# Expert routing beside a streamed projection: fewer and partly bfloat16 operations, maxima from the finished map, more steps a load

## The chip, the core and the metric

The kernel runs on one core of a Trainium2 chip. The metric is the time of one execution in microseconds of the device, taken as the median of several runs. The core has five engines with a queue each: TensorE (PE in the profile, its weight loads PEld), VectorE (DVE), ScalarE (ACT), GpSimd (POOL) and SyncE (SP, which here only issues DMAs). An engine executes its queue in order and waits at semaphores for the others.

## What is computed

One layer of a diffusion backbone for 256 latent tokens (and 256 context tokens) of width 2048: modulated RMSNorm, one input projection into an mLSTM and a differential attention, a gated merge, an output projection with residual, and then PEER, a retrieval among 128 x 128 = 16384 single-neuron experts. All work around the change lies in PEER:

```
q = (h @ w_pq).reshape(B, T, 8 heads, 2, 128)
s = einsum('bthpd,hpnd->bthpn', q, sub_keys)            # 128 scores per head and half
s1, i1 = top_k(s[..., 0, :], 16);  s2, i2 = top_k(s[..., 1, :], 16)
cand_s = s1[..., :, None] + s2[..., None, :]             # 256 candidates per head
top_s, pos = top_k(cand_s, 16)                           # 16 experts per head
idx = (i1 * 128 + i2)[pos];  g = softmax(top_s)
act = gelu(einsum('td,ted->te', h, expert_u[idx]))       # 128 experts per token
out = einsum('te,ted->td', g * act, expert_v[idx])
```

The result goes through a gated residual and a last RMSNorm.

## The kernel before

The kernel does not gather `expert_u`. It multiplies all 16384 rows of it with all 256 tokens ("the U stage"), and builds in the meantime a map of the gates, 16384 x 256, which is zero wherever a token did not choose an expert. The product of both weighs the rows of `expert_v` ("the V stage"). Of `expert_v` only those rows are read that some token of a group uses; which ones is worked out by `lists`.

The U stage is the loop `for i1 in range(0, P, 2)` over 64 pairs of key rows (from L1616). `u_pair` takes four pieces of 128 x 1024 float32 for a pair with `take()`: a piece is loaded by a DMA on SP's queue (L117), rounded to `hi` on ACT (L133), and its rest `lo` is subtracted on DVE, every fourth time on POOL (L136). `raw`, `hi` and `lo` have three buffers each. Then come 16 matmuls for the piece, eight with `hi` and 512 columns and eight with `lo` and 256 (L93, tile `s`), held in program order by `mp_`. After a pair DVE adds the halves (L1625), ACT takes the GELU (L1626), and ACT's queue writes the 128 x 512 result to `ag_dram` in DRAM (L1630).

Everything else in this stage is a chain of Python generators in the list `back`, begun by what `best` has left to do and then `plan`. After each piece `pump(pace[0])` runs `pace[0]` steps on average, where a step goes to the next `yield`. So `pace` and the `yield`s fix where the matmuls of the routing lie between those of U, since both are kept in program order; so are the DMAs of U's pieces, the gate map's and the gathers, each on its queue. The remaining instructions are placed by a planner with a time model of its own, which may move an instruction of DVE, ACT or POOL ahead of others that are not ready. The steps of `plan`:

- `best`: scores of the halves on PE, and their 16 best with `top16` (MAX8, FIND_INDEX8, MATCH_REPLACE8, twice).
- `retrieve(t)` for each of two tiles of 128 tokens: sums of candidates on POOL (L1170), `top16` over 256, softmax, and the two indices of each choice, found by a comparison with 0..15 (L1194, DVE), a product (L1196, POOL) and a sum (L1200, DVE); three transposes bring them to `i1T`, `i2T`, `gT` (L1207, L1208).
- `gate_map(t)`: for each token a matmul of two one-hots (`one_hots`, L1234), four tokens to a step. ACT makes the first one-hot with Abs and Relu (L1237, L1238), DVE and POOL in turn the second, which carries the gate (L1241). ACT copies the result from PSUM to the tile `gates` (L1279); DVE takes its maximum over the four tokens (L1283) and merges it into `most` for the group of 32 tokens (L1285). `gate_map(0)` is woven with `retrieve(1)`.
- `map_out`: each half of a map (64 tokens) leaves in eight DMAs of 512 KB on SP's queue (L1253), in pieces of 256 bytes, beside the next half; the last is run out by `plan`.
- `lists`: from `most`, which blocks of expert rows are needed and where they go: ten `fill`s (matmuls with triangular and full ones, scans on DVE, products on POOL), then one-hots for 126 columns, four to a step (L1408, L1409 on DVE, L1411 on ACT, L1412 on POOL), and 126 matmuls that add them up to index lists.
- `soon`: fetches eight blocks of `expert_v` by indirect DMAs on POOL's queue (L1501), waits until `made[0]` has reached `EARLY` = 104 slices of U, and then does the first five items of the V stage.

At the 63rd pair `drain()` runs all that is left of `plan`. The paces are 1.05 (L1448), 1.6 for the fills (L1461), 1.15 for the one-hots of `lists` (L1415) and 1.3 for `soon` (L1464).

## Time and profile before

| | us |
|---|---|
| timed runs, median of 3 (lowest to highest) | 2327.84 (2323.7 to 2328.26) |
| profiled execution, its own time | 2340.29 |
| its span, first to last instruction | 2338.4 |
| PE busy in the span | 2198.0 |
| DVE busy | 1570.3 |
| ACT busy | 1057.4 |
| POOL busy | 935.0 |
| U's first and last matmul start at | 1168.1 and 2048.6 |

The profile is of one execution. Busy is the time in which an engine's instructions run, one after another or overlapped. Of an instruction that waited, the trace names the one that released it ("<-"). Matmuls are pipelined, so two that follow each other overlap in the rows. An instruction is named by its line in the kernel; U's matmuls and those of the routing share L93, since both go through `mp_`, and are told apart by their tiles (`s` for U, `g` for the routing, `v` for the V stage).

### The profile page before, as it was taken

To read this page: it belongs to the slowest core of one execution; us is meant where nothing else is said; L and a number is where in the kernel's file an instruction comes from. 1 tells how busy PE (TensorE), PEld (TensorE's weight loads), DVE (VectorE), ACT (ScalarE), POOL (GpSimd) and SP (SyncE) were. 2 spreads that over 40 slices of the span, in tenths; PEclk is the share of its full clock that TensorE was granted. 3 is DMA by queue.
4 is the path that set the end of the run, shared out by engine and by line. 5 is a ranking of instruction groups with operands and counts; after the bars stand their busy time and mean duration, and the time that the engine had idled before them with its cause. 6 is when DMAs were issued, how large, how long until landed. Compare 5 with 4: busy or idle time off the path is not lost.

```text
span 2338.4 us, 37404 instructions
## 1 busy us (share of the span) xinstructions
PE 2198.0 (94%) x14184; PEld 1880.2 (80%) x14184; DVE 1570.3 (67%) x2760; ACT 1057.4 (45%) x1723; POOL 935.0 (40%) x957
## 2 busy tenths in 40 slices
PE   6999999999999999998999999999999989999994
PEld 3669988999899999887987888888787776756661
DVE  3357973767876858746799766876799944454553
ACT  3232232244566744444444777995335433333431
POOL 2132210236534200002235755772456454566553
PEclk9999999999999999998999999999999999999997
DMA  9968964866456588755556457878665588899895
GB/s 380 351 212 304 332 228 134 316 206 192 144 150 203 169 280 283 272 191 176 172 174 209 160 183 222 229 213 238 197 194 172 184 330 321 330 414 387 333 395 190
DMA packets 235910, 570.98 MB, mean 244 GB/s; under 512 B 85154, under 2 KB 118739, under 8 KB 221264
## 3 DMA queue, kind: packets, MB, share of 16 engines
q1 hardware_dynamic: 153888, 339.34, 44.1%
q0 software_dynamic: 46992, 211.67, 25.1%
q10 hardware_dynamic: 34848, 17.57, 2.6%
q8 instruction: 111, 1.82, 0.3%
q14 instruction: 71, 0.58, 0.1%
HBM read 524.33 MB, written 38.93 MB: 241 GB/s over the span
## 4 chain that ended last, share of the span: by engine, by line
PE 69%; DVE 12%; DMA 6%; issue 5%; ACT 3%; POOL 2%; ACTq 0%; another core or an unknown queue 0%; SPq 0%; DVEq 0%; POOLq 0%
PE acc L289 24%; PE s L93 18%; PE acc L278 11%; PE v L93 9%; DVE lo L136 4%; DMA raw<-expert_u 3%; PE g L93 2%; ACT hi L133 2%; PE m L433 1%; DMA vraw<-expert_v,idxV 1%; PE m L278 1%; DMA raw<-w_mod 1%; DVE at L1409 1%; DVE act L1625 1%; PE m L382 1%
## 5 line engine op out<-in xcount | busy, mean ns | idle before, releaser
L133 ACT CAST hi<-raw 128x1024 fp32r<-128x1024 f32 x528 | 551.6, 1048 | 803.9 <-PE acc L289 256.7
L136 DVE TENSOR_TENSOR lo<-raw,hi 128x1024 fp32r<-128x1024 f32 x457 | 599.7, 1316 | 283.6 <-ACT hi L133 279.2
L93 PE MATMUL s<-h,hi 128*128 128x512 f32 x2048 | 743.3, 404 | 3.2 <-ACT hi L133 2.6
L93 PE MATMUL s<-h,lo 128*128 128x256 f32 x2048 | 581.3, 284 | 33.2 <-DVE lo L136 20.8
L93 PEld LDWEIGHTS s<-h,hi 128*128 128x128 f32 x2048 | 388.6, 190 | 96.0 <-ACT hi L133 6.3
L93 PEld LDWEIGHTS s<-h,lo 128*128 128x128 f32 x2048 | 390.7, 191 | 45.5 <-DVE lo L136 28.6
L289 PE MATMUL acc<-hL,hi 128*128 128x256 f32 x2048 | 421.7, 286 | 0.0
L289 PEld LDWEIGHTS acc<-hL,hi 128*128 128x128 f32 x2048 | 342.5, 193 | 1.5
L289 PE MATMUL acc<-hL,lo 128*128 128x256 f32 x1024 | 292.3, 286 | 4.6 <-DVE lo L136 4.6
L136 POOL TENSOR_TENSOR lo<-raw,hi 128x1024 fp32r<-128x1024 f32 x71 | 176.9, 2492 | 254.3 <-ACT hi L133 248.6
L289 PEld LDWEIGHTS acc<-hL,lo 128*128 128x128 f32 x1024 | 197.5, 193 | 6.2 <-DVE lo L136 5.5
L117 POOL DMA_DIRECT2D raw<-w_mod x128 | 68.2, 533 | 300.2 <-DVE raw L522 278.7
L522 DVE SCALAR_TENSOR_TENSOR raw<-raw,cr 128x1024 f32<-128x1024 f32 x128 | 154.7, 1219 | 32.4 <-DMA raw<-w_mod 17.6
L1241 POOL TENSOR_SCALAR o<-iota,i1T,gT 128x128 f32<-128x128 f32 x128 | 138.9, 1092 | 93.1 <-PE g L93 49.3
L1517 DVE TENSOR_TENSOR lo<-vraw,hi 128x1024 fp32r<-128x1024 f32 x74 | 90.3, 1228 | 100.5 <-ACT hi L1515 76.1
L1501 POOL DMA_INDIRECT vraw<-expert_v,idxV x99 | 106.6, 1077 | 97.7 <-PE v L93 38.1
L289 PE MATMUL acc<-hC,hi 128*128 128x256 f32 x512 | 134.0, 283 | 0.0
L1515 ACT CAST hi<-vraw 128x1024 fp32r<-128x1024 f32 x74 | 77.1, 1049 | 115.0 <-PE v L93 56.1
L93 PE MATMUL v<-hi,l 128*128 128x512 f32 x448 | 123.5, 394 | 4.0 <-issue 3.1
L1625 DVE TENSOR_REDUCE act<-s 128x256 f32<-128x512 f32 x126 | 86.2, 684 | 53.6 <-PE s L93 48.2
L1501 POOL DMA_INDIRECT ag<-ag_dram,idxG x99 | 106.3, 1074 | 33.6 <-issue 27.3
L93 PE MATMUL v<-vraw,w 128*32 128x512 f32 x640 | 90.2, 642 | 28.5 <-DVE w L1536 12.9
(427 smaller groups left out, 3859.9 us busy)
## 6 DMA issues: line engine op xcount, KB each, us to landing
raw<-expert_u SPq DMA_DIRECT2D x256, 512.0 KB
raw<-w_in SPq DMA_DIRECT2D x176, 512.0 KB
raw<-w_mod POOLq DMA_DIRECT2D x128, 512.0 KB
raw<-w_mod SPq DMA_DIRECT2D x64, 512.0 KB
raw<-w_out SPq DMA_DIRECT2D x32, 512.0 KB
raw<-w_pq SPq DMA_DIRECT2D x32, 512.0 KB
ag_dram<-gates SPq DMA_DIRECT2D x32, 512.0 KB
ag_dram<-act ACTq DMA_DIRECT2D x126, 128.0 KB
```

The source lines that it names most:

```text
L93: tc.keep_in_program_order(mm(*args, **kw))
L117: d = queue.dma_start(r, src)
L133: nc.scalar.copy(h, r)
L136: (nc.vector if shared[0] else nc.gpsimd).tensor_tensor(l, r, h.bitcast(F32), op=OP.subtract)
L278: mm(acc[ti], lhsT=lhs(sa, ti, 2 * kp + k2), rhs=hl[sb][:, k2 * 512:(k2 + 1) * 512], start=first and k2 == 0 and i == 0, stop=last and k2 ...
L289: mm(acc[c][:, g * T:(g + 1) * T], lhsT=hl[sb][:, k2 * 512 + c * P:k2 * 512 + (c + 1) * P], rhs=rhs(sa, g, k), start=first and k2 == 0 and ...
L522: product = nc.vector.scalar_tensor_tensor(r, r, 1.0, cr, op0=OP.mult, op1=OP.mult, accum_out=part[:, h, i:i + 1])
L1241: (nc.gpsimd if i % 2 else nc.vector).tensor_scalar(o2[:, i, 0:width], iota[:, 0:width], cols[:, i:i + 1], factor[:, i:i + 1], op0=OP.is_e ...
L1501: tc.keep_in_program_order(nc.gpsimd.indirect_dma_start(out=out, out_offset=None, in_=src, in_offset=bass.IndirectOffsetOnAxis(ap=idx[:, b ...
L1515: nc.scalar.copy(h, raw)
L1517: nc.vector.tensor_tensor(l, raw, h.bitcast(F32), op=OP.subtract)
L1625: nc.vector.reduce_sum(act[:, e], ps.rearrange("p s t -> p t s"), axis=AX.X)
```

## The change

- `top16` yields after its first round. In `retrieve` a step therefore ends in the middle of a head; in `best` nothing changes.
- `retrieve` looks up the two indices without POOL: positions and indices are copied to bfloat16 with the heads innermost, and for each of the two indices DVE compares 16 x 16 x 8 elements, multiplies as many, and adds in a tree of 1024, 512, 256 and 128 elements. It has 17 steps in place of 23.
- `one_hots`: all four second one-hots of a group are made on DVE (two on DVE and two on POOL before). The first one-hot is made on ACT for every second group, for the others by one comparison of 512 elements on DVE.
- The maxima for `most` are no longer taken from PSUM for each group of four tokens. `map_out` takes them from the finished tile `gates`, 16 rows and two groups of 32 tokens at a time (1024 elements), right after the DMA of these rows. `map_out` has 8 steps and a last one in place of 16 and one, and is stepped at every second group, from the second on.
- `lists`: the sums over kinds in `fill` become additions in bfloat16; the one-hots are in bfloat16 with the four columns innermost, both operands too, and the product with `column` is on DVE instead of POOL. The matmuls read their four columns with a step of four elements. `hots` always makes four columns; the last group overlaps the one before.
- `pace` is 1.3 from the beginning (1.05 before) and 1.7 for the one-hots of `lists` (1.15 before).

```diff
@@ top16, best
             if r == 0:
                 nc.vector.match_replace(src, v, src, NEG)
+                yield
+
+    iota8 = tkr.tile([P, 16, HEADS], BF16, name="iota8")
+    nc.vector.tensor_copy(iota8, b3(iota[:, 0:16], HEADS))
...
@@ retrieve
-        tif = tk.tile([P, 16, 16], F32, name="tif", tag="tif", bufs=1)
-        nc.vector.tensor_copy(tif, ti[t])
+        tib = tk.tile([P, 2, 16, HEADS], BF16, name="tib", tag="tib", bufs=1)
+        nc.vector.tensor_copy(tib, ti[t].rearrange("p (h s) j -> p s j h", s=2))
...
-            top16(cs.rearrange("p a b -> p (a b)"), gv[:, h, :], gp[:, h, :])
-            yield
+            for _ in top16(cs.rearrange("p a b -> p (a b)"), gv[:, h, :], gp[:, h, :]):
+                yield
...
         nc.vector.tensor_tensor(e, e, b3(z, 16), op=OP.mult)
+        yield
...
-        posf = tk.tile([P, 2, HEADS, 16], F32, name="posf", tag="posf", bufs=1)
-        nc.vector.tensor_copy(posf, pos)
+        posb = tk.tile([P, 2, 16, HEADS], BF16, name="posb", tag="posb", bufs=1)
+        nc.vector.tensor_copy(posb, pos.rearrange("p s h k -> p s k h"))
         yield
         ii = []
+        every = [P, 16, 16, HEADS]
         for s in range(2):
+            oh = tk.tile(every, BF16, name="oh", tag="oh", bufs=1)
+            nc.vector.tensor_tensor(oh, posb[:, s].unsqueeze(1).to_broadcast(every),
+                                    iota8.unsqueeze(2).to_broadcast(every), op=OP.is_equal)
+            yield
+            nc.vector.tensor_tensor(oh, oh, tib[:, s].unsqueeze(2).to_broadcast(every), op=OP.mult)
+            yield
+            for w in (8, 4, 2):
+                nc.vector.tensor_tensor(oh[:, 0:w], oh[:, 0:w], oh[:, w:2 * w], op=OP.add)
             r = tk.tile([P, HEADS, 16], F32, name="ix", tag=f"ix{s}", bufs=1)
-            for h in range(HEADS):
-                if h % 4 == 0:
-                    four = tk.tile([P, 4, 16, 16], F32, name="oh", tag="oh", bufs=1)
-                oh = four[:, h % 4]
-                nc.vector.tensor_tensor(oh, b3(posf[:, s, h, :], 16),
-                                        iota[:, 0:16].unsqueeze(1).to_broadcast([P, 16, 16]), op=OP.is_equal)
-                nc.gpsimd.tensor_tensor(oh, oh, ti4[:, h, s, :].unsqueeze(1).to_broadcast([P, 16, 16]),
-                                        op=OP.mult)
-                if h % 4 == 3:
-                    yield
-                    nc.vector.reduce_sum(r[:, h - 3:h + 1], four, axis=AX.X)
-                if h % 2:
-                    yield
+            nc.vector.tensor_tensor(r.rearrange("p h k -> p k h"), oh[:, 0], oh[:, 1], op=OP.add)
             ii.append(r)
-        yield
+            yield
...
@@ one_hots
+        if on_act:
+            for i in range(4):
+                nc.scalar.activation(o1[:, i], iota, AF.Abs, bias=rows[:, i:i + 1], scale=-1.0)
+            nc.scalar.activation(o1, o1, AF.Relu, bias=ones[:, 0:1], scale=-1.0)
+        else:
+            nc.vector.tensor_tensor(o1, b3(rows, P), iota.unsqueeze(1).to_broadcast([P, 4, P]), op=OP.is_equal)
...
-        for i in range(n):
-            (nc.gpsimd if i % 2 else nc.vector).tensor_scalar(o2[:, i, 0:width], iota[:, 0:width], cols[:, i:i + 1], factor[:, i:i + 1],
+        for i in range(4):
+            nc.vector.tensor_scalar(o2[:, i], iota, cols[:, i:i + 1], factor[:, i:i + 1],
                                     op0=OP.is_equal, op1=OP.mult)
...
@@ map_out
-        for i in range(0, P, 8):
+        for i in range(0, P, 16):
             g, j = gates[i // 64], i % 64
-            if i % 16 == 0:
-                tc.keep_in_program_order(nc.sync.dma_start(rows[:, i:i + 16, w], g[:, j:j + 16, :]))
+            tc.keep_in_program_order(nc.sync.dma_start(rows[:, i:i + 16, w], g[:, j:j + 16, :]))
+            nc.vector.reduce_max(most[:, 4 * t + 2 * hf_:4 * t + 2 * hf_ + 2, i:i + 16].rearrange("p g i -> p i g"),
+                                 g[:, j:j + 16, :].rearrange("p i (g c) -> p i g c", g=2), axis=AX.X)
             yield
...
@@ gate_map
-            return one_hots(i2T[:, w], i1T[:, w], gT[:, w])
+            return one_hots(i2T[:, w], i1T[:, w], gT[:, w], q // 4 % 2)
...
-                top = most[:, 4 * t + at // 32 - (at % 32 == 0), :]
-                new = gm.tile([P, P], F32, name="new", tag="new", bufs=2) if (at - 4) % 32 else top
-                nc.vector.reduce_max(new, ps.rearrange("p t i -> p i t"), axis=AX.X)
-                if new is not top:
-                    nc.vector.tensor_tensor(top, top, new, op=OP.max)
-                step(leaving)
+                if q % 8:
+                    step(leaving)
                 yield
...
@@ lists, fill
-            nc.vector.reduce_sum(gone[:, 0:w], pw.rearrange("p c i -> p i c"), axis=AX.X)
+            if n == 4:
+                nc.vector.tensor_tensor(half_gone[:, :, 0:w], pw[:, 0:2], pw[:, 2:4], op=OP.add)
+                pw2 = half_gone[:, :, 0:w]
...
+                nc.vector.tensor_tensor(gone[:, 0:w], pw2[:, 0], pw2[:, 1], op=OP.add)
...
@@ lists, hots
+            i = min(i, N_LIST - 4)
+            w = slice(i, i + 4)
+            o1 = ls.tile([P, P, 4], BF16, name="h1", tag="h1", bufs=3)
+            o2 = ls.tile([P, 2, N_BLOCKS, 4], BF16, name="h2", tag="h2", bufs=3)
+            at = ls.tile([P, N_BLOCKS, 4], BF16, name="at", tag="at", bufs=2)
+            nc.vector.tensor_tensor(o1, hl[:, 1, w].unsqueeze(1).to_broadcast([P, P, 4]), iota4, op=OP.is_equal)
+            nc.vector.tensor_tensor(at, hl[:, 0, w].unsqueeze(1).to_broadcast([P, N_BLOCKS, 4]), iota4[:, 0:N_BLOCKS],
+                                    op=OP.is_equal)
+            nc.scalar.activation(o2[:, 0], at, AF.Copy, scale=row)
+            nc.vector.tensor_tensor(o2[:, 1], at, column[:, w].unsqueeze(1).to_broadcast([P, N_BLOCKS, 4]), op=OP.mult)
...
-        pace[0] = 1.15
+        pace[0] = 1.7
...
-                mp_(sums, lhsT=o1[:, j], rhs=o2[:, j], start=i + j == 0, stop=i + j == N_LIST - 1)
+            for j in range(max(0, i + 4 - N_LIST), 4):
+                mp_(sums, lhsT=o1[:, :, j], rhs=o2[:, :, :, j], start=i + j == 0, stop=i + 4 >= N_LIST and j == 3)
...
@@ plan
-    pace = [1.05]
+    pace = [1.3]
```

More of the change, by code (lines that the diff above doesn't have):

```diff
@@ L1140, in best @@
             for i in range(4):
-                top16(sc[:, i, :], tv[t][:, 4 * blk + i, :], ti[t][:, 4 * blk + i, :])
+                for _ in top16(sc[:, i, :], tv[t][:, 4 * blk + i, :], ti[t][:, 4 * blk + i, :]):
+                    pass
                 yield
@@ L1161, in retrieve @@
     def retrieve(t):
-        tif = tk.tile([P, 16, 16], F32, name="tif", tag="tif", bufs=1)
-        nc.vector.tensor_copy(tif, ti[t])
+        tib = tk.tile([P, 2, 16, HEADS], BF16, name="tib", tag="tib", bufs=1)
+        nc.vector.tensor_copy(tib, ti[t].rearrange("p (h s) j -> p s j h", s=2))
         tv4 = tv[t].rearrange("p (h s) i -> p h s i", s=2)
-        ti4 = tif.rearrange("p (h s) i -> p h s i", s=2)
         gv = tk.tile([P, HEADS, 16], F32, name="gv", tag="gv", bufs=1)
@@ L1231, in build, with one_hots @@
     i1T, i2T, gT = slots
-    def one_hots(rows, cols, factor, n=4, width=P):
+    def one_hots(rows, cols, factor, on_act):
         o1 = gm.tile([P, 4, P], F32, name="o1", tag="o1", bufs=3)
-        for i in range(n):
-            nc.scalar.activation(o1[:, i], iota, AF.Abs, bias=rows[:, i:i + 1], scale=-1.0)
-        nc.scalar.activation(o1[:, 0:n], o1[:, 0:n], AF.Relu, bias=ones[:, 0:1], scale=-1.0)
+        if on_act:
[4 more added lines that the diff above has]
+            nc.vector.tensor_tensor(o1, b3(rows, P), iota.unsqueeze(1).to_broadcast([P, 4, P]), op=OP.is_equal)
         o2 = gm.tile([P, 4, P], F32, name="o2", tag="o2", bufs=3)
-        for i in range(n):
-            (nc.gpsimd if i % 2 else nc.vector).tensor_scalar(o2[:, i, 0:width], iota[:, 0:width], cols[:, i:i + 1], factor[:, i:i + 1],
+        for i in range(4):
+            nc.vector.tensor_scalar(o2[:, i], iota, cols[:, i:i + 1], factor[:, i:i + 1],
                                     op0=OP.is_equal, op1=OP.mult)
@@ L1308, in lists @@
         nc.vector.tensor_scalar(row, row, 1.0, None, op0=OP.add)
+        iota4 = ls.tile([P, P, 4], BF16, name="iota4")
+        nc.vector.tensor_copy(iota4, b3(iota, 4))
         column = ls.tile([P, N_LIST], BF16, name="column")
@@ L1334, in lists @@
         nc.gpsimd.memset(places, 0.0)
-        gone = ls.tile([P, N_LIST], F32, name="gone")
+        gone = ls.tile([P, N_LIST], BF16, name="gone")
+        half_gone = ls.tile([P, 2, N_LIST], BF16, name="half_gone")
         blocks_at = ls.tile([P, 16, 4], F32, name="blocks_at")
@@ L1392, in lists @@
         placei = ls.tile([P, 3, N_LIST], I32, name="placei")
-        hl = ls.tile([P, 2, N_LIST], F32, name="hl")
-        nc.vector.reduce_sum(gone, places.rearrange("p c i -> p i c"), axis=AX.X)
-        nc.vector.tensor_scalar(placei[:, 2], gone, float(NOWHERE), None, op0=OP.add)
+        hl = ls.tile([P, 2, N_LIST], BF16, name="hl")
+        nc.vector.reduce_sum(zero, places.rearrange("p c i -> p i c"), axis=AX.X)
+        nc.vector.tensor_scalar(placei[:, 2], zero, float(NOWHERE), None, op0=OP.add)
         nc.vector.tensor_scalar(placei[:, 1], placei[:, 2], P - 1, None, op0=OP.bitwise_and)
@@ L1425, in lists @@
                 ready.append(hots(i + 8))
-            for j in range(min(4, N_LIST - i)):
-                mp_(sums, lhsT=o1[:, j], rhs=o2[:, j], start=i + j == 0, stop=i + j == N_LIST - 1)
+            for j in range(max(0, i + 4 - N_LIST), 4):
+                mp_(sums, lhsT=o1[:, :, j], rhs=o2[:, :, :, j], start=i + j == 0, stop=i + 4 >= N_LIST and j == 3)
             yield
```

15 lines of the change are left out of this document (5 added, 10 removed).

## The prediction

> **What bounds the kernel now.** I read the page first, then the windows of the U stage, beside which the routing runs: all engines (PE, PE's weight load, DVE, ACT and POOL busy, then granted clock, DMA share, GB/s), and PE's instructions on the tile `s`, which count U's matmuls.
>
> ```profile
> span 2338.4 us, 37404 instructions
> ...
> PE 69%; DVE 12%; DMA 6%; issue 5%; ACT 3%; POOL 2%; ACTq 0%; another core or an unknown queue 0%; SPq 0%; DVEq 0%; POOLq 0%
> ```
>
> ```profile
> 1168.00:1302.00 134.00, 122.64 (x686) 106.17 (x685) 122.35 (x306) 63.34 (x77) 72.67 (x58) 0.96 0.57 180
> 1302.00:1598.00 296.00, 291.67 (x1832) 260.20 (x1831) 213.56 (x358) 242.84 (x535) 186.24 (x182) 0.99 0.72 207
> 1598.00:1648.00 50.00, 45.83 (x251) 38.16 (x250) 26.83 (x36) 17.65 (x21) 7.19 (x3) 1.00 1.00 271
> 1648.00:1763.00 115.00, 108.37 (x601) 91.25 (x600) 103.39 (x133) 44.28 (x46) 61.24 (x41) 0.99 0.60 190
> 1763.00:1868.00 105.00, 99.06 (x610) 82.54 (x609) 100.71 (x106) 53.38 (x70) 56.65 (x40) 1.00 0.52 170
> 1868.00:2050.00 182.00, 168.31 (x988) 130.56 (x986) 78.43 (x106) 58.10 (x61) 90.19 (x69) 0.99 0.89 328
> ```
>
> ```profile
> 1168.00:1302.00 134.00, 119.90 (x655) 0.96 0.57 180
> 1302.00:1598.00 296.00, 249.00 (x1317) 0.99 0.72 207
> 1598.00:1648.00 50.00, 45.83 (x251) 1.00 1.00 271
> 1648.00:1763.00 115.00, 107.38 (x581) 0.99 0.60 190
> 1763.00:1868.00 105.00, 93.50 (x483) 1.00 0.52 170
> 1868.00:2050.00 182.00, 149.91 (x818) 0.99 0.89 328
> ```
>
> I call the rows A (scores, `retrieve(0)`), B (both gate maps, with `retrieve(1)`), C (the last map leaves), D (fills of `lists`), E (its one-hots), F (`soon`). PE sets the time, but DVE is nearly as full in A (91%), D (90%) and E (96%). What PE needs without waits comes from the chain of waits and from the groups:
>
> ```profile
> 1302.48 0.89 PE g L93 x8
> 1303.38 5.65 PE s L93 x32
> 1309.03 0.89 PE g L93 x8
> ```
>
> ```profile
> L93 PE MATMUL g<-skT,qT 128*128 128x128 f32 x24 | 3.2, 275 | 0.0
> L93 PE MATMUL v<-vraw,w 128*32 128x512 f32 x168 | 19.3, 596 | 0.0
> L93 PE MATMUL g<-h,h 128*128 128x198 bf16 x126 | 15.8, 251 | 1.9 <-DVE h L1408 1.9
> ```
>
> A *load* is one piece of U, 16 matmuls, 2.82 us; a group of four gate-map columns is 0.89. A: 655/16 loads are 115.5, with scores and transposes 119.5, so 14.5 of 134 are lost. B: 232 + 64 x 0.89 = 289, lost 7. C: 44.2, lost 5.8. D: 102.4 and about 4.6 for its small matmuls (an estimate), lost 8. E: 85.1 + 15.8, lost 4.1. F: 144 + 19, lost 19. The change adds and removes no matmul, so these 58 us are all that the stage can win.
>
> **Steps against loads.** After each load `pump` runs `pace` steps. Before: 16 left over from `best`, 23 of `retrieve(0)`, 57 of `gate_map(0)` woven with `retrieve(1)`, 34 of `gate_map(1)`, 17 of `map_out` are 147, at 1.05 in 140 loads; 56 of the fills at 1.6 in 35; 35 of the one-hots at 1.15 in 30.4; together 205.4. The trace agrees: A to E hold 3287 matmuls, 205.4 loads. After: 16 + 17 + 51 + 34 + 9 = 127 at 1.3 in 97.7 loads, then 35, then 35 at 1.7 in 20.6: 153.3. But `soon`, once eight rows are fetched, waits for 104 slices of U, load 208, in either kernel (before, its row steps end at load 212). So 52 loads of earlier routing become some 48 bare loads of U and about 4 loads' start for `soon`. PE's total stands; only what lies beside its work is packed differently.
>
> **DVE in A to C.** Before, it has 122.35 + 213.56 + 26.83 = 363 us in 480 (76%).
>
> ```profile
> L136 DVE TENSOR_TENSOR lo<-raw,hi 128x1024 fp32r<-128x1024 f32 x195 | 265.3, 1363 | 101.5 <-ACT hi L133 97.4 <-issue 4.0
> L1625 DVE TENSOR_REDUCE act<-s 128x256 f32<-128x512 f32 x126 | 86.2, 684 | 53.6 <-PE s L93 48.2 <-issue 4.6 <-DMA raw<-expert_u 0.4
> L1241 DVE TENSOR_SCALAR o<-iota,i1T,gT 128x128 f32<-128x128 f32 x128 | 42.4, 373 | 43.2 <-PE g L93 42.9
> L1283 DVE TENSOR_REDUCE new<-g 128x128 f32<-128x512 f32 x56 | 38.3, 683 | 6.2 <-ACT gates L1279 5.5
> L1285 DVE TENSOR_TENSOR most<-most,new 128x128 f32<-128x128 f32 x56 | 29.1, 519 | 1.7
> L1194 DVE TENSOR_TENSOR oh<-posf,iota 128x256 f32<-128x256 f32 x32 | 20.2, 679 | 0.1
> L1200 DVE TENSOR_REDUCE ix<-oh 128x64 f32<-128x1024 f32 x8 | 9.7, 1207 | 0.9 <-POOL oh L1196 0.9
> ```
>
> ```profile
> L1382 DVE TENSOR_TENSOR single<-single,put x2: 381/430/480, 1710.5 to 1732.8; 128x416 bf16<-128x416 bf16 x2
> ```
>
> ```profile
> L1369 DVE TENSOR_TENSOR use<-use,kp x1: 679/679/679, 1605.6 to 1605.6; 128x504 f32<-128x504 f32 x1
> ```
>
> U's own part is 0.75 `lo` (about 1.2 us alone) and half a reduction (0.68) a load, 1.25: 41.2 loads fewer take 52 off. In `retrieve`, L1194 and L1200 (29.9) go. In their place stand, twice for each of two tiles, two bf16 operations of 2048 elements, a tree of 1024, 512 and 256, and a last add of 128. The trace has no such broadcast in bf16. The bounds: at the f32 pace (679 ns for 504, 1207 for 1024, so 1.0 ns an element and 0.15 us fixed) 4 x 7.2 = 29 us; at the pace of L1382's fastest (381 ns for 416, 0.55 ns an element) 4 x 4.1 = 16.5. I take 16.5, the only row in which all operands are bf16. The gate map drops L1283 (38.3, and eight more of the same, 5.4) and L1285 (29.1); its L1241 doubles to 256 (+42.4); 32 groups of four compare 512 elements on DVE (0.68 by L1369, +22); 32 maxima over 1024 finished elements (1.21 by L1200, +39). Sum: 363 - 52 - 29.9 + 16.5 - 72.8 + 103.4 = 328 us, beside 97.7 x 2.82 + 57 + 4 = 337 of PE. DVE goes from 76% to 97%: the DVE work saved is less than the loads taken away.
>
> **What leaves GpSimd and ACT.**
>
> ```profile
> L1241 POOL TENSOR_SCALAR o<-iota,i1T,gT 128x128 f32<-128x128 f32 x128 | 138.9, 1092 | 93.1 <-PE g L93 49.3 <-issue 39.9 <-DVE act L1625 1.9
> L1196 POOL TENSOR_TENSOR oh<-oh,tif 128x256 f32<-128x256 f32 x32 | 31.8, 1020 | 17.7 <-DVE oh L1194 17.7
> ```
>
> POOL falls from 266 us in A to C to about 70 (its ten fewer `lo` of 2.4 us counted). ACT loses half of its 64 one-hot groups, some 64 us; at 243 of 296 in B it sets nothing now, so I count nothing for it. POOL was not the bound either, but it made waits: DVE's operations stood behind it.
>
> ```profile
> 1475.06 2.41 POOL L136 TENSOR_TENSOR lo<-raw,hi 128x1024 fp32r<-128x1024 f32 x1
> ```
>
> ```profile
> 1475.07 2.54 DVE L1285 TENSOR_TENSOR most<-most,new 128x128 f32<-128x128 f32 x1
> ```
>
> That maximum costs 0.29 alone and 2.54 when it starts with POOL's `lo`. [...]
>
> **The sum, stretch by stretch.** Where DVE was over 90% full, PE lost 4% (E), 7% (D) and 11% (A). For A and B after I bound the loss so: 4% to 11% of 318 us of PE are 13 to 35 against 21.5 now. I take A's 28 loads (80 us and 4) at 11%, 9, since its chain through transposes stays, and the rest (234) at E's 4%, 9.6, the row nearest in DVE's share: -3. C: eight maps of 512 KB go out in 7 loads where they had 16. E gives a load 0.52 x 105/30.2 = 1.81 us of DMA; C's 50 us full then leave 2.7 for a map. 8 x 2.7 + 7 x 1.81 = 34 against 20 of PE; three buffers hide two loads (5.6), so some 9 are lost for 5.8: +3 (without cover +9). The map's first DMA also holds SP's queue:
>
> ```profile
> 1525.30 1.04 SPq L117 DMA_DIRECT2D raw<-expert_u  x1
> 1539.25 0.40 SPq L1253 DMA_DIRECT2D ag_dram<-gates  x1
> ```
>
> U's loads queue behind it for 13 us until ACT has copied the half's last group. It now comes one group later, so the hold is up to 3 us shorter; I count 0. D: nine reductions (about 1.0 us) become bf16 adds of 252 and 126 (0.5), -2.5. E has three bf16 operations on DVE for a group (0.43 + 0.36 + 0.36 by L1382's pace) against two of
>
> ```profile
> L1408 DVE TENSOR_TENSOR h<-hl,iota 128x512 bf16<-128x512 f32 x31 | 29.3, 954 | 0.0
> L1409 DVE TENSOR_TENSOR at<-hl,iota 128x396 bf16<-128x396 f32 x31 | 28.7, 934 | 0.0
> ```
>
> so 37 us and U's 26 beside 58 + 16 = 74 of PE; from 96% full to 85% I leave 1.5 lost, -2.6. Its matmuls now read weights and columns at a step of four elements, which no row shows: between nothing and as much again (15.8); I take nothing, since bytes and count stay. F: three to four loads earlier; PE waited at U's end for rows that the last steps ask for:
>
> ```profile
> 2061.09 3.59 PE L93 MATMUL v<-vraw,w 128*32 128x512 f32 x26 [3.55 <-DMA vraw<-expert_v,idxV]
> ```
>
> Between 0 and -10; I take -3. The 48 bare loads cost their 2.82 each, and the burst of eight row gathers moves there with its wait.
>
> In all -3 + 3 - 2.5 - 2.6 - 3 = -8. The profiled execution took 2340.3 (span 2338.4), so 2332; the timed median is 12.5 lower, and with the same distance I predict 2320.
>
> **Rivals.** *GpSimd made most of the waits* (faster): A falls to its transposes' waits (5), B to 3, D to 3, E to 1.5, F to 14, C stays: 32 lost for 58, 2302. For it: the wait of 17.7 us between L1194 and L1196, and 2.54 above. Against it: DVE at 97%. *DVE becomes the bound of `gate_map(1)`* (slower): a load with 1.3 groups asks 1.25 + 1.3 x (4 x 0.34 + 0.34 + 0.61) = 4.25 us of DVE and 2.82 + 1.3 x 0.89 = 3.98 of PE. It decides as soon as operations don't overlap, and then 26 loads lose 7 us, and 6.5 `lo` on POOL 2.4 each, 16; net of the rest -8, +15: 2343. Against it: neighbouring DVE operations overlap by some 0.07 us in the rows above. *The early finish is paid back in C* (no change): nothing covers the maps' DMAs, +9 for +3, 2326. *The bf16 operations don't run faster*, rows of eight and four read again: `retrieve` +13, E's DVE 84 against 74 of PE: with half of `retrieve` hidden, +16 to the sum, 2336. Only L1382, without such rows, speaks against it. [...]
>
> **How the numbers follow.** Forecast 0.42, GpSimd 0.22, DVE bound 0.15, paid back in C 0.14, no bf16 gain 0.07. No change is within 0.2%, 4.7 us, about what a measurement of this kernel can tell. The forecast's own range is 2311 to 2329, seven parts in ten of it faster; with the first rival and some of the third, 0.55 faster; 0.25 the same, from the rest of the forecast and of the third; 0.20 slower. The range goes a little past the GpSimd rival and close to the full price of the DVE rival: 2298 to 2342.
>
> **What would show it.** DVE some 90% busy or more from 1168 on, with about 1250 us where the first gate group stands (load 28.5); one-hots of `lists` done near load 153; POOL without L1241; a stretch of about 48 loads at 2.82; PE's waits on `lo` in the gate maps as long as before. It would be wrong if 2048 bf16 elements take 2.2 us, if PE waits for `o` throughout `gate_map(1)`, or if PE waits less than 5 us in the gate maps.

## The result and the profile after

The changed kernel takes 2347.81 us (median of 4 runs, 2344.34 to 2350.25), the kernel before took 2325.77 beside it (4 runs, 2318.92 to 2328.26). The ratio is 1.0094, with a 95% interval of 1.0073 to 1.0116: slower by 22 us, where 2320 was forecast with a range of 2298 to 2342.

```profile
span 2344.7 us, 37075 instructions
```

The profiled execution of the changed kernel took 2346.8 us. That of the kernel before lay 14.5 us above its timed median, and the V part behind U's end took between 262 and 300 us in the profiles of this case, also on different chips; so the two profiles are compared stretch by stretch within the U stage. From U's first matmul to its last it lasted 880.4 us before and 913.9 after: 33.5 longer. By the timed median the kernel before has about 275 us behind U's end in place of its profile's 290 (an estimate: 2326 less 2, 1168 and 880), the changed one has 262, so some 12 of the 33 come back there.

The windows of the changed kernel, cut at the first and last instruction of each stretch (A scores, B gate maps, C last map leaves, D fills, E one-hots of the lists, F bare loads and `soon`): length, busy time of PE, PE's weight load, DVE, ACT and POOL, granted clock, DMA share, GB/s.

```profile
1169.20:1259.60 90.40, 84.26 (x478) 72.61 (x477) 87.09 (x253) 41.29 (x47) 28.16 (x18) 0.98 0.56 180
1259.60:1512.90 253.30, 240.28 (x1514) 215.16 (x1513) 225.62 (x423) 171.71 (x365) 41.48 (x53) 0.97 0.70 195
1512.90:1557.80 44.90, 36.68 (x189) 30.73 (x188) 29.21 (x36) 13.34 (x14) 6.69 (x3) 0.92 0.95 257
1557.80:1668.80 111.00, 97.31 (x535) 81.20 (x534) 104.31 (x145) 40.34 (x43) 54.66 (x40) 0.98 0.54 174
1668.80:1743.50 74.70, 74.70 (x415) 59.99 (x416) 58.44 (x113) 37.59 (x53) 12.50 (x5) 0.98 0.45 148
1743.50:2083.40 339.90, 320.10 (x1827) 262.26 (x1825) 141.60 (x173) 119.87 (x127) 122.40 (x82) 0.99 0.76 268
```

The same windows for U's matmuls alone (tile `s` on PE): length, busy time and count, clock, DMA share, GB/s.

```profile
1169.20:1259.60 90.40, 81.73 (x448) 0.98 0.56 180
1259.60:1512.90 253.30, 194.75 (x999) 0.97 0.70 195
1512.90:1557.80 44.90, 36.68 (x188) 0.92 0.95 257
1557.80:1668.80 111.00, 96.16 (x514) 0.98 0.54 174
1668.80:1743.50 74.70, 57.70 (x289) 0.98 0.45 148
1743.50:2083.40 339.90, 302.60 (x1664) 0.99 0.76 268
```

As in the prediction, what a stretch loses is its length less 2.82 us for each 16 of these matmuls and less the routing's own matmuls (A 4.8, B 58, D 4.6, E 15.8, F 19 us, the same for every kernel here, so that a matmul that gets longer shows as a loss). B, for example: 253.3 - 999/16 x 2.82 - 58 = 19.2. Cut in the same manner, the kernel before gives figures up to 1.1 us from the prediction's.

| us lost | A | B | C | D | E | F | sum | U stage |
|---|---|---|---|---|---|---|---|---|
| before | 13.7 | 5.9 | 5.8 | 8.1 | 4.0 | 17.9 | 55.3 | 880.4 |
| after | 6.6 | 19.2 | 11.8 | 15.8 | 8.0 | 27.6 | 89.0 | 913.9 |
| difference | -7.1 | +13.3 | +6.0 | +7.7 | +4.0 | +9.7 | +33.7 | +33.5 |

The loads fell as foreseen: the first gate group stands at load 28.0, and A to E hold 152.4 loads for 205. Only A gained. B, C, D, E and F each lost, so no single cause can carry the result. Not all of a loss is waiting: in B PE is busy for 240.3 of 253.3 us, so 13.0 of the 19.2 are waits. The other 6.2 are matmuls that took longer (U's 414 and 287 ns on the mean for 407 and 282 before), at a granted clock of 0.97 for 0.99. The groups of the changed kernel in which the main operations are seen (busy us and mean ns of one; then idle time before them and its releaser):

```profile
L1246 DVE TENSOR_SCALAR o<-iota,i1T,gT 128x128 f32<-128x128 f32 x256 | 93.7, 425 | 7.5 <-PE g L93 7.3
L1256 DVE TENSOR_REDUCE most<-gates 128x32 f32<-128x1024 f32 x32 | 36.5, 1207 | 0.6 <-ACT gates L1283 0.6
...
L1196 DVE TENSOR_TENSOR oh<-posb,iota 128x2048 bf16<-128x2048 bf16 x4 | 4.9, 1215 | 0.0
L1199 DVE TENSOR_TENSOR oh<-oh,tib 128x2048 bf16<-128x2048 bf16 x4 | 4.9, 1214 | 0.0
...
L93 PE MATMUL g<-h,h 128*128 128x198 bf16 x126 | 25.8, 357 | 1.9 <-DVE h L1422 1.9
```

And PE's waits within B of the changed kernel:

```profile
L93 PE MATMUL s<-h,lo 128*128 128x256 f32 x497 | 142.5, 287 | 6.6 <-DVE lo L136 6.6
...
L93 PE MATMUL g<-o,o 128*128 128x128 f32 x511 | 66.4, 277 | 4.6 <-DVE o L1246 4.6
```

Two things stand out: PE now waits for DVE in the gate maps, and the 126 list matmuls became 0.11 us longer each.

### The profile page after: what moved, and what is told of

It is laid out like the page before. It is cut to its first block, busy times and chain, and to the rows that moved or that the text cites. A ratio compares the mean times of both kernels' runs of the same rounds, so it can differ in the third digit from the quotient of the medians.

```text
span 2344.7 us, 37075 instructions
## 1 busy us (share of the span) xinstructions
PE 2203.1 (94%) x14184; PEld 1891.6 (81%) x14184; DVE 1570.7 (67%) x2858; ACT 1002.1 (43%) x1563; POOL 723.2 (31%) x765
## 5 line engine op out<-in xcount | busy, mean ns | idle before, releaser
L133 ACT CAST hi<-raw 128x1024 fp32r<-128x1024 f32 x528 | 551.6, 1048 | 913.7 <-PE s L93 260.9
L136 DVE TENSOR_TENSOR lo<-raw,hi 128x1024 fp32r<-128x1024 f32 x457 | 578.5, 1269 | 308.6 <-ACT hi L133 307.7
L93 PEld LDWEIGHTS s<-h,lo 128*128 128x128 f32 x2048 | 395.6, 193 | 49.2 <-DVE lo L136 39.2
L278 PE MATMUL acc<-hi,hL 128*128 128x512 f32 x320 | 110.0, 403 | 0.5 <-ACT hi L133 0.5
L289 PE MATMUL acc<-h,hi 128*128 128x256 f32 x512 | 98.9, 294 | 4.8 <-ACT hi L133 3.7
```

What stands on the lines that cost most here:

```text
L93: tc.keep_in_program_order(mm(*args, **kw))
L133: nc.scalar.copy(h, r)
L136: (nc.vector if shared[0] else nc.gpsimd).tensor_tensor(l, r, h.bitcast(F32), op=OP.subtract)
L278: mm(acc[ti], lhsT=lhs(sa, ti, 2 * kp + k2), rhs=hl[sb][:, k2 * 512:(k2 + 1) * 512], start=first and k2 == 0 and i == 0, stop=last and k2 ...
L289: mm(acc[c][:, g * T:(g + 1) * T], lhsT=hl[sb][:, k2 * 512 + c * P:k2 * 512 + (c + 1) * P], rhs=rhs(sa, g, k), start=first and k2 == 0 and ...
```

## The experiments

Each kernel is the one before or the changed one with one edit. "U" is the U stage, in us; ratios are to the kernel before. Some were timed in rounds and have an interval; of the others a single profile is read by stretches, which shows U's length and not the time of the whole. Stretches that an edit leaves alone differ between profiles: B lost 17.4 to 19.2 in six, F 24.8 to 29.0 in eight, and E 6.6 or 6.7 in those with the changed one-hots, beside the 8.0 above. So a difference below 2 us in B or below 4 in F says nothing.

### Is it the pace? (e1, e2)

e1 is the changed kernel with the old pace, e2 the kernel before with the new one.

```diff
-    pace = [1.3]
+    pace = [1.05]
-        pace[0] = 1.7
+        pace[0] = 1.15
```

> The changed kernel with the paces of before (1.05, and 1.15 for the one-hots of lists); every operation is as changed. Theory 'packing': the 22 us are lost because 1.3 steps a load fill DVE and crowd the DMAs; with the old paces the time is at most that of before, 2315 to 2327, and the gate maps lose under 15 us for 27. Theory 'operations': the new operations themselves cost PE time, above all the matmuls of the lists that read with a step of four elements (their rows went from 249 to 358 ns), and the additions that wait for GpSimd; then it stays 12 us or more above before, 2338 or more.

> The kernel before with the paces of after (1.3, and 1.7 for the one-hots of lists) and nothing else. Packing: DVE's 363 us for scores and gate maps then stand beside 110 loads instead of 140, the one-hots' 100 us beside 20 loads; 15 us or more slower than before, 2341 or more, and slower than the changed kernel, whose operations are lighter. Operations: about as before, 2320 to 2332.

| us lost | A | B | C | D | E | F | sum | U | ratio (95%) |
|---|---|---|---|---|---|---|---|---|---|
| e1 | 9.4 | 16.3 | 11.6 | 15.4 | 6.7 | 29.4 | 88.8 | 913.7 | 1.0098 (1.0070 to 1.0125) |
| e2 | 15.3 | 7.5 | 5.3 | 10.4 | 10.1 | 28.9 | 77.7 | 902.4 | 1.0064 (1.0035 to 1.0093) |

At the old pace the changed kernel is just as slow, so packing the operations closer isn't what costs B to D. Yet the new pace alone makes the kernel before slower, by E (DVE 98% busy) and above all by F: 28.9 for 17.9. F is dear in both, and what they share is that the lists are done well before load 208. In e2 the gate maps lose 7.5 at the new pace, so B's 19.2 must come from the changed operations.

### The step of four elements (e3, e11)

The kernel before, with the list one-hots laid out so that the matmuls read them with a step of four elements: weights and columns (e3), or the columns alone (e11, the second line).

```diff
-            o1 = ls.tile([P, 4, P], BF16, name="h1", tag="h1", bufs=3)[:, 0:n]
-            o2 = ls.tile([P, 4, 2, N_BLOCKS], BF16, name="h2", tag="h2", bufs=3)[:, 0:n]
+            o1 = ls.tile([P, P, 4], BF16, ...).rearrange("p c j -> p j c")[:, 0:n]
+            o2 = ls.tile([P, 2, N_BLOCKS, 4], BF16, ...).rearrange("p s b j -> p j s b")[:, 0:n]
```

> The kernel before, only the two one-hot tiles of lists laid out with the four columns innermost, so that the 126 matmuls read weights and columns with a step of four elements; values, types and operations stay. Operations: each of the 126 matmuls takes some 0.08 us longer as in the changed kernel (25.8 us busy for 15.8), so 8 to 12 us slower than before. Packing, or an effect of the other types: within 4 us of before, and the rows stay near 250 ns.

> The kernel before, only the tile of the 198 moving columns of lists laid out with the four groups innermost; the weights' tile, which DVE writes and PE loads, stays dense. If the moving side is what slows the 126 matmuls, they take 350 ns or more for 249, and the weight loads stay at 98 ns for 117; with the weights' tile dense DVE keeps its 0.95 us for the first one-hot, and the one-hots' stretch loses 12 to 18 us for 4. If the weights are the cause, the matmuls stay under 270 ns.

Groups of e3:

```profile
L1408 DVE TENSOR_TENSOR h<-hl,iota 128x512 bf16<-128x512 f32 x31 | 51.2, 1677 | 0.0
...
L93 PE MATMUL g<-h,h 128*128 128x198 bf16 x126 | 27.2, 356 | 1.5 <-DVE h L1408 1.2 <-POOL h L1412 0.3
```

Tile `h` of e11 (least, median and longest ns, first and last start):

```profile
L93 PE MATMUL g<-h,h x126: 335/356/359, 1773.3 to 1872.8; 128*128 128x198 bf16 x126
...
L93 PEld LDWEIGHTS <-h x126: 95/115/119, 1773.3 to 1872.6; 128*128 128x128 bf16 x126
```

In e3 E lost 21.1 us, but not by PE alone: the same edit makes DVE, ACT and POOL write with that step, and L1408 went from 954 ns to 1677, so DVE stayed 97% busy over a longer stretch. (Ratio 1.0084, 1.0055 to 1.0112.) e11 leaves the weights dense, and the matmul is as long as in e3 and in the changed kernel: 356 ns for 251. So the moving operand's step is what costs, 0.105 x 126 = 13 us by the single matmuls, 10 to 11 by the groups' busy time (15.8 to 25.8 in the changed kernel, 27.2 in e3), since neighbours overlap. E's loss in e11 is 7.3 for 4.0: PE as a whole was busy 8.0 us longer there (98.6 for 90.6), but its waits fell from 5.9 to 1.2, since the longer matmuls fill time in which it had waited for DVE. The weight load became longer in e11 too (115 ns for 98), with dense weights, so the weights' layout isn't what makes it longer.

A step of four elements, 8 bytes, thus made the matmul with that moving operand 42% longer (356 ns for 251).

### The sums of the fills (e4)

The changed kernel with the one reduction of the kernel before in place of the bfloat16 additions.

```diff
-            if n == 4:
-                nc.vector.tensor_tensor(half_gone[:, :, 0:w], pw[:, 0:2], pw[:, 2:4], op=OP.add)
...
-                nc.vector.tensor_tensor(gone[:, 0:w], pw2[:, 0], pw2[:, 1], op=OP.add)
+            nc.vector.reduce_sum(gone[:, 0:w], pw.rearrange("p c i -> p i c"), axis=AX.X)
```

> The changed kernel, only the sums over kinds in the fills made again by one reduction with one input instead of additions with two. Operations: the additions stand behind GpSimd's products (994 ns for 126 elements), the reduction does not; the fills lose 8 us as before instead of 14, so 4 to 7 us faster than the changed kernel, 2341 to 2344. Packing: no difference beyond 3 us.

D lost 8.1 us, the others as in the changed kernel: sum 78.6, U 903.7, ratio 1.0057 (1.0027 to 1.0086). What the reduction takes in the kernel before, by its group (none of this line took longer than 1.085 us):

```profile
L1360 DVE TENSOR_REDUCE gone<-put 128x126 f32<-128x504 bf16 x6 | 6.4, 1074 | 0.1
```

The two additions that replace it in the changed kernel, by their groups:

```profile
L1370 DVE TENSOR_TENSOR gone<-half_gone 128x126 bf16<-128x126 bf16 x6 | 6.0, 994 | 0.1
...
L1363 DVE TENSOR_TENSOR half_gone<-put 128x252 bf16<-128x252 bf16 x6 | 4.2, 701 | 0.1
```

One addition on its time line, on DVE and on POOL (start, us):

```profile
1577.39 1.28 DVE L1370 TENSOR_TENSOR gone<-half_gone 128x126 bf16<-128x126 bf16 x1
```

```profile
1577.26 1.32 POOL L1373 TENSOR_TENSOR places<-places,rank 128x504 f32<-128x504 f32 x1
```

POOL's product began 0.13 us ahead and both end together within 0.1 us. Over its eight instructions of 104 or 126 elements the addition took (least, median, longest ns):

```profile
L1370 DVE TENSOR_TENSOR gone<-half_gone x8: 210/1108/1279, 1564.7 to 1640.9; 128x126 bf16<-128x126 bf16 x6, 128x104 bf16<-128x104 bf16 x2
```

It took 0.21 us the one time it began ahead of POOL's product (1564.70 and 1564.71). The other seven took 0.93 to 1.28 us, and each ended 0.06 to 0.09 us behind the end of one of POOL's. PE's waits in D are for DVE's `lo`, in the changed kernel and then in e4:

```profile
L93 PE MATMUL s<-h,lo 128*128 128x256 f32 x256 | 73.1, 286 | 7.9 <-DVE lo L136 7.6 <-POOL lo L136 0.2
```

```profile
L93 PE MATMUL s<-h,lo 128*128 128x256 f32 x257 | 73.2, 285 | 2.3 <-DVE lo L136 2.1 <-POOL lo L136 0.2
```

The reduction of the kernel before also ran beside POOL's products (one from 1668.58 to 1669.66, POOL's from 1667.60 to 1669.54): 1074 ns for it, 994 + 701 for the two smaller additions.

### The gate maps (e5, e6, e13, e14, e16)

Five versions of the changed kernel with parts of `gate_map` as before the change: the maxima group by group from PSUM (e5; with one buffer `new` where the kernel before has two), half of the second one-hots on GpSimd (e6), the first one-hot always on ACT (e13), e6 and e13 together (e14), all three (e16, with e5's one buffer).

```diff
@@ e5, e16
+                nc.vector.reduce_max(new, ps.rearrange("p t i -> p i t"), axis=AX.X)
+                if new is not top:
+                    nc.vector.tensor_tensor(top, top, new, op=OP.max)
@@ e6, e14, e16
-            nc.vector.tensor_scalar(o2[:, i], iota, cols[:, i:i + 1], factor[:, i:i + 1],
+            (nc.gpsimd if i % 2 else nc.vector).tensor_scalar(o2[:, i], iota, ...
@@ e13, e14, e16
-            return one_hots(i2T[:, w], i1T[:, w], gT[:, w], q // 4 % 2)
+            return one_hots(i2T[:, w], i1T[:, w], gT[:, w], True)
```

> The changed kernel, only the maxima taken per group of four columns from PSUM and merged, as before (to make room, one buffer for the maximum of a group instead of two, and the two halves of a sum share a tile with a later one). The gate maps of the changed kernel lose 19 us of PE beside 6 before; with the new paces alone they lost 7.5. 'DVE too full': this adds 64 reductions of 0.68 us and 56 merges and drops 32 of 1.21, so DVE goes from 89% to 95% or more of the gate maps and they lose more, 22 us or more. 'The long reduction over the finished map is what U's pieces queue behind': the loss falls under 13.

> The changed kernel, only every second of the four second one-hots of a group made on GpSimd again. 'DVE too full': DVE falls from 225 to about 185 us in the gate maps, and they lose 10 us or less for 19, although GpSimd and DVE stand in each other's way again. 'GpSimd's share is no help' (the two engines block each other, as I argued from the 2.54 us maximum): the loss stays at 17 or more.

> The changed kernel with the first one-hot of every group on ACT, as before the change (half of them were one DVE comparison of 512 elements, 0.75 us by L1243). B lost 19.2 us there. Theory that DVE's added one-hots make B's loss: DVE in B falls from 225 to about 202 us and the loss to 8 to 13. Rival, that it is the order on DVE (long operations ahead of U's `lo`: maxima of 1.2 us and four one-hots in a row) and not how full DVE is: B stays above 15, as it did at 72% of DVE when half the second one-hots were moved to GpSimd (15.1).

> The changed kernel with both one-hots of a group made where they were before the change: the first on ACT, the second half on GpSimd; the maxima from the finished map and the new `retrieve` stay. If the one-hots make B's loss: B at 7.5 or less, what the kernel before loses at the same pace with DVE 78% busy; DVE here about 155 us of 245. If the late maxima make it: B still 12 or more, with PE waiting for `lo` from DVE. If a part each: between.

> The changed kernel with the whole gate map as before the change: the first one-hot on ACT, half of the second on GpSimd, the maxima group by group from PSUM; the new `retrieve`, the pace and the eight steps of the map's output stay. B lost 19.2 us in the changed kernel and 13.4 with the one-hots alone undone. If what is left is the late maxima (1.2 us each on DVE, ahead of U's `lo`): B at 4 to 8, where the kernel before has 7.5 at this pace. If it comes with the pace and the new `retrieve`: B still 12 or more.

| | one-hots | maxima | B lost | DVE busy in B | U |
|---|---|---|---|---|---|
| after | new | late | 19.2 | 89% | 913.9 |
| e5 | new | from PSUM | 24.6 | 95% | 916.1 |
| e13 | first as before | late | 19.6 | 80% | 915.6 |
| e6 | second as before | late | 15.1 | 72% | 908.7 |
| e14 | both as before | late | 13.4 | 66% | 905.1 |
| e16 | both as before | from PSUM | 6.2 | 82% | 902.1 |

B of e14 (window of all engines; then PE's wait for `lo` within it), and the same of e16:

```profile
1265.70:1513.20 247.50, 237.96 (x1514) 213.04 (x1513) 164.08 (x256) 217.60 (x513) 160.72 (x175) 0.99 0.72 200
...
L93 PE MATMUL s<-h,lo 128*128 128x256 f32 x499 | 141.7, 284 | 7.5 <-DVE lo L136 7.5
```

```profile
1261.10:1501.40 240.30, 235.17 (x1514) 210.48 (x1513) 196.70 (x349) 217.44 (x514) 168.99 (x175) 1.00 0.74 206
...
L93 PE MATMUL s<-h,lo 128*128 128x256 f32 x499 | 140.0, 281 | 0.0
```

With all three undone B is back at the loss of the kernel before (5.9), at the new pace and with the new `retrieve`. Undoing both one-hots is worth 5.8 us, the late maxima then 7.2. And DVE's busy share isn't the measure: e14 has DVE 66% busy and loses 13.4, e16 has it 82% busy and loses 6.2. The maxima from PSUM take more of DVE (0.68 us 64 times and 0.4 us 56 times, for 1.2 us 32 times), and PE waits for `lo` no more. Why late maxima delay `lo` is seen on the time lines of DVE and PE (start and length in us; in brackets the wait). The changed kernel, then e14:

```profile
1404.04 9.09 DVE L1256 TENSOR_REDUCE most<-gates 128x32 f32<-128x1024 f32 x8
...
1413.19 1.21 DVE L136 TENSOR_TENSOR lo<-raw,hi 128x1024 fp32r<-128x1024 f32 x1
```

```profile
1414.46 0.39 PE L93 MATMUL s<-h,lo 128*128 128x256 f32 x1 [2.82 <-DVE lo L136]
```

```profile
1402.26 9.09 DVE L1256 TENSOR_REDUCE most<-gates 128x32 f32<-128x1024 f32 x8
```

```profile
1413.41 0.39 PE L93 MATMUL s<-h,lo 128*128 128x256 f32 x1 [3.14 <-DVE lo L136]
```

The eight maxima of a half don't run one by one with the eight steps of `map_out`. Only the DMAs are held in program order; the maxima stand on DVE in one row of 9.1 us as soon as the half is finished, and U's `lo` behind them. In B of the changed kernel this happens at 1349.6, 1404.0 and 1461.8 (there seven, and one more behind four one-hots). PE's waits at the end of these three rows, for `o` (3.59 and 0.99 us) and for `lo` (0.76, 2.82 and 3.04), are 11.2 of B's 13.0 us of waits. In e14 three waits for `lo` at the same places make 7.5 of 9.5 us, and in e16 no wait is longer than 0.97. No run holds the maxima to their steps, so what that alone would save isn't measured.

With the new one-hots the maxima from PSUM made B worse (e5), so the parts don't add up singly. There PE's wait for `lo` also falls, from 6.6 to 1.9 us, but its wait ahead of the gate map's matmuls grows from 4.6 to 13.8, and 11.3 of these end with a maximum (L1284): with DVE 95% busy, the maximum that has to read a group's PSUM tile comes late. e6 lies between what its two theories asked for. e13 alone gave nothing: it took 23 us off DVE and left the loss.

### When the map leaves (e8)

The changed kernel with 16 steps in `map_out` and a step at every group, as before.

```diff
             g, j = gates[i // 64], i % 64
+            yield
             tc.keep_in_program_order(nc.sync.dma_start(rows[:, i:i + 16, w], g[:, j:j + 16, :]))
...
-                if q % 8:
-                    step(leaving)
+                step(leaving)
```

> The changed kernel, only that the map's DMAs are spread over 16 steps again, one DMA for two steps, so that the last eight leave in 13 loads instead of 7. If the crowd of map DMAs behind gate_map(1) is what costs there, the loss between the last gate group and the first fill falls from 12 to 5 or 6 us, as with the new paces alone (5.3); if it is the late reductions of the map, it stays at 10 or more.

SP's DMAs in C of the changed kernel (start and length in us, queue, line):

```profile
1512.62 0.40 SPq L1255 DMA_DIRECT2D ag_dram<-gates  x1
1513.12 1.07 SPq L117 DMA_DIRECT2D raw<-expert_u  x1
1514.24 4.33 SPq L1255 DMA_DIRECT2D ag_dram<-gates  x2
...
1534.70 0.45 SPq L1255 DMA_DIRECT2D ag_dram<-gates  x1
```

Eight maps of 512 KB leave in 22 us, between U's own loads; the granted clock was 0.92 in the stretch. With 16 steps C's loss is that of the kernel before, and D gets a little better too; C's window for U's matmuls in e8:

```profile
1515.90:1572.90 57.00, 51.28 (x284) 1.00 0.89 249
```

57.0 - 284/16 x 2.82 = 6.9 lost (sum 77.9, U 902.6). e1, at the slower pace but with eight steps, lost 11.6, so it is the steps' number that decides. It isn't the late maxima: e5 and e16 have none and lost 10.7 and 12.3 in C.

### The rows and the wait for load 208 (e7, e9, e10, e15)

In `soon` eight row gathers are issued, then it waits for load 208. e7 is the changed kernel with the gathers behind the wait. e15 leaves them where they are and adds eight empty steps behind the wait. e9 is the kernel before with the new `retrieve` (and `top16`, `iota8`) alone, e10 is e9 with e7's edit.

```diff
@@ e7, e10
                 rows = []
+                while made[0] < EARLY:
+                    yield
                 for b in work[0] + work[1]:
                     rows.append(stage_rows(*b))
                     yield
-                while made[0] < EARLY:
-                    yield
@@ e15, behind the wait
+                for b in rows:
+                    yield
```

> The changed kernel, only that soon waits for the 104 slices of U first and fetches its eight blocks of rows then, as it came out before. From the end of lists to the end of U the changed kernel loses 28 us of PE, the kernel before 18, and so do all that finish lists early. If the burst of eight gathers of 1 MB in the middle of U is a cost of its own, the loss here falls to 18 to 21, with no loss between the end of lists and load 208; the V stage gets nothing from the change, so the span is 5 to 10 us shorter. If U alone loses time when it runs bare, the loss stays at 26 or more.

> The kernel before with the new retrieve alone (bfloat16 look-up on DVE, yields inside the heads), old paces. If the new look-up is the part of the change that gains, the stretch up to the first gate group loses 7 to 9 us for 13.7. But it has 12 steps less, so lists end near load 194 and the eight row gathers run 14 loads ahead of the wait: by the theory of the early burst the rest of U then loses 22 to 28 us for 18, and the time is within 5 us of before. If the early burst is nothing, 5 to 8 us faster than before.

> As the run before, and soon fetches its rows after the wait. Theory of the early burst: the rest of U loses 12 to 15 us, as when only this was put back into the changed kernel (12.1), U takes 866 to 875 us, and the time is 5 to 15 us less than before, the fastest of all. If the early burst is nothing, the same as the run before.

> The changed kernel with eight empty steps in `soon` after its wait for load 208; the burst of eight row gathers stays where it is, right behind the lists. It tells apart why fetching the rows after the wait took 15 us off F. Theory that the eight steps ahead of the rest did it, by putting the later gathers and V groups further apart from the wait: the burst near 1750 still loses about 10 us, F falls from 27.6 to 14 to 17. Theory that it was the place of the burst: F stays at 25 to 28.

U's matmuls in F of the changed kernel: the burst of gathers, the bare loads, and the rest.

```profile
1744.00:1790.00 46.00, 38.49 (x203) 0.98 0.84 327
1790.00:1900.00 110.00, 110.00 (x619) 0.99 0.65 210
1900.00:2084.00 184.00, 153.78 (x843) 0.99 0.80 289
```

The burst loses 46 - 203/16 x 2.82 = 10 us. The bare loads take about their 2.82 (619/16 of them make 109 of the 110 us). From 1900 on 184 - 148.6 - 19 = 16.4 are lost. What the burst does is seen on ACT's time line, where each cast is the start of one load (in brackets its wait and the releaser):

```profile
1771.92 1.05 ACT L133 CAST hi<-raw 128x1024 fp32r<-128x1024 f32 x1 [2.15 <-DMA raw<-expert_u]
1775.82 1.05 ACT L133 CAST hi<-raw 128x1024 fp32r<-128x1024 f32 x1 [2.85 <-DMA raw<-expert_u]
1779.72 1.05 ACT L133 CAST hi<-raw 128x1024 fp32r<-128x1024 f32 x1 [2.85 <-DMA raw<-expert_u]
1783.61 1.05 ACT L133 CAST hi<-raw 128x1024 fp32r<-128x1024 f32 x1 [2.84 <-DMA raw<-expert_u]
```

U's pieces arrive every 3.9 us while 8 MB of rows come in beside them: 1.1 us lost a load. F's window for U's matmuls in e7, in e15, in e9 and in e10:

```profile
1748.70:2073.10 324.40, 298.76 (x1664) 0.98 0.78 270
```

```profile
1742.70:2068.30 325.60, 299.13 (x1664) 0.99 0.78 270
```

```profile
1828.60:2052.60 224.00, 189.10 (x1024) 0.97 0.85 309
```

```profile
1824.70:2035.90 211.20, 185.23 (x1024) 0.98 0.85 302
```

By the same working these lose 12.1 (e7), 13.3 (e15), 24.5 (e9) and 11.7 (e10). The first reading, that e7 gains by taking the burst out of the middle of U, fell with e15: the burst stays, and F falls as far. U's matmuls in e15, the burst and all that follows:

```profile
1742.70:1790.00 47.30, 39.88 (x209) 0.98 0.85 321
1790.00:2068.30 278.30, 259.25 (x1457) 1.00 0.77 261
```

The burst still loses 10.5 us, the rest 278.3 - 256.8 - 19 = 2.5. In e7 the burst costs as much in its new place (10.1 us between 1900 and 1960). So what falls is the 16.4 from 1900 on, by the eight steps by which the later gathers and V groups stand further behind the wait: PE's waits for `hi` and `lo` there were 12.3 us in the changed kernel and are 1.5 in e15. In the kernel before the row steps themselves end at load 212, four loads behind the wait's. Part comes back: behind U's end e10 had 8.5 us more than e9 in the profiles (299.8 and 291.3), and of 15.5 us saved in U the medians show 7.6.

e9 has ratio 0.9998 (0.9977 to 1.0020), U 882.8: the new `retrieve` saves 6.7 in A and B together and loses 6.6 in F, since the lists are done earlier. e10 has 0.9964 (0.9947 to 0.9982), U 867.3, 2340.05 us against 2348.73 beside it: by the ratios it beats both kernels.

### Three edits undone together (e12)

The changed kernel with the edits of e4, e7 and e8.

> The changed kernel with three things as before at once: the fills' sums by reduction, the map's DMAs over 16 steps, the rows fetched after the wait; gate map, one-hots and paces stay as changed. If the three losses add up (7.7, 4.9 and 15.5 us), U loses some 61 us for 89 and takes about 886 us, and the time is within 6 us of before. If they hide each other, U stays above 892.

C lost 6.4, D 8.5, F 16.3, the rest as in the changed kernel: 63.4 in all, U 888.5, ratio 1.0051 (1.0029 to 1.0074). In U the three parts are separate causes that add up nearly fully (25.6 us for 28.1), and B and E are left. The timed runs don't show all of it: e4 alone has 1.0057 with a U that is 15 us longer. The V part behind U's end took 300 us in e12's profile and 291 in e4's, so more than half of that gain was paid back there.

## Why the prediction was wrong, point by point

| step | predicted, us | measured | settled by |
|---|---|---|---|
| A and B | -3 | +6.2 (A -7.1, B +13.3) | e5, e6, e13, e14, e16 |
| C | +3 | +6.0 | e8 |
| D | -2.5 | +7.7 | e4 |
| E | -2.6 | +4.0 | e11; e3 in part |
| F | -3 | +9.7 | e7, e15, e2, e9, e10 |
| sum | -8 | +33.7 | |

- **Loads against steps held.** The gate groups began at load 28.0 (28.5 predicted), the lists were done at 152.4 (153.3), the bare loads took 2.84. POOL had 76 us in A to C for the 70 foreseen. DVE had 342 us there for 328.
- **The bfloat16 lookup held.** 2048 elements took 1.21 us; the pace that the prediction took from a row without broadcasts (0.55 ns an element and 0.15 us) makes 1.28. The rival without a gain there falls. The small additions behind them did not hold: those of 256 elements took 0.75 us on the mean and the last ones, of 128, 1.17, so the four look-ups took 23.8 us of DVE for 16.5.
- **A was right, and better than taken:** 6.6 lost for 9, nearer the 5 of the first rival.
- **B failed at "the rest (234) at E's 4%, 9.6, the row nearest in DVE's share".** DVE's share was taken as the measure of PE's loss, and e14 beside e16 shows that it isn't. What sets it is where DVE's operations stand ahead of `lo` and `o`: the edit lets eight maxima run in a row at the end of each half, and PE's waits behind them are 11.2 of B's 13.0 us; undoing the one-hots is worth 5.8. The rival of DVE as the bound named the engine, the waits for `o` among them, and a price of 23 us for B's second half; B as a whole lost 13 more. Its condition, that DVE is full, isn't the one that decides (the overlap of 0.07 us that was set against it stands in the time lines, not in the rows shown there). The 2.4 us for each `lo` on POOL in its price was an estimate from the one pair of rows at 1475; no run shows it as a price of PE's time. In the changed kernel four one-hots on DVE took 3.20 us beside such a `lo` (1496.5) and 1.10 with POOL idle (1365.2), and none of PE's waits in B ends with POOL. Of the signs that the prediction named, "PE's waits on `lo` in the gate maps as long as before" is the one that failed here: 1.0 us before, 6.6 after.
- **C was right in kind, and its term half the size:** +6.0 for +3, within the bound of +9 without cover. The hold on SP's queue, counted as 0, isn't told apart from the maps' DMA time.
- **D failed at "nine reductions (about 1.0 us) become bf16 adds of 252 and 126 (0.5), -2.5".** (Nine times 0.5 us off DVE would be 4.5; why 2.5 was taken isn't said.) The pair took 1.7 us on the mean, not 0.5. The prediction had the rows that show a two-input operation on DVE stand behind POOL (2.54 us for 0.29) and did not apply them to this edit, which sets two such operations beside POOL's products in place of one reduction that stayed at or below 1.085 us there.
- **E failed at "I take nothing, since bytes and count stay".** The bound stood there, 0 to 15.8; the matmuls' busy time grew by 10 us, and the stretch lost 4.0 more (2.7 by the other profiles). The DVE part was right in kind: 78% busy for 97%, with PE busy all through the stretch.
- **F failed at "three to four loads earlier", -3.** The burst did move to the bare loads, and its wait was called moved with it, but its price was counted nowhere: 10 us, where the kernel before lost some 6 between 1865 and 1905. And the steps behind the wait were taken to gain by coming earlier; they lost 16.4 from 1900 on, for some 12 before, and eight steps later they lose little (e15). Why a distance of eight steps matters so much isn't settled.
- **Rival one** (GpSimd made most of the waits) came near in A and fell in the rest. In the gate maps, work taken off GpSimd cost more on DVE than it freed (B lost 19.2 us, 15.1 with half of it back on GpSimd, e6). In D, DVE did stand behind GpSimd, but by additions (0.93 to 1.28 us for 0.21) that the edit itself put there.

Of the 41.7 us between the predicted sum and the measured one, 32.1 lie in A and B, D and F. There the prediction priced each edit by the time that an engine gives or saves, and left the order in which the work stands as it was. That turned its sign.

## What to carry to other kernels

Taking work off an engine that isn't the bound pays only if what takes its place doesn't stand ahead of the operations that the bound engine waits for; look for these waits, not for the busy share (e14, e16). Operations that aren't held to their steps can run in one row when their input is ready, however the steps are spread (the eight maxima). Side work that ends at a fixed wait gains nothing by getting there sooner; look at what it leaves behind the wait (e10, e15). Price a layout that suits one engine at every engine that reads or writes the tile (e3, e11).

## What the runs showed of the hardware that was not expected

- A bfloat16 moving operand with a step of four elements: 356 ns for 251 with 198 columns, weights dense or not.
- Writing bfloat16 with that step (e3 beside the kernel before): DVE 954 to 1677 ns for 512 elements, ACT 631 to 1208, POOL 1106 to 1644 for 396.
- DVE's reduction of 504 elements took 1.07 us on the mean beside POOL's products and never above 1.085, an addition of a quarter of that between 0.21 and 1.28.
- The granted clock in the stretches in which PE waited in short pieces (8.2 of C's 44.9 us, 13.0 of B's 253.3): 0.92 in C of the changed kernel, 0.97 in its B, where the kernel before had 1.00 and 0.99. Right behind two of the waits in B it was 0.53 (1365 to 1369) and 0.51 (1474.5 to 1478), and U's matmuls took 0.41 and 0.63 us there for 0.28 and 0.40. Behind the wait of 2.82 us at 1414.5 it stayed at 1.00.
